# Opening of an mLSTM layer: operands by channel pairs, the prompt's norm factor inside the second range, the decay scans moved behind the key copies

## The chip, the cores and the metric

The kernel runs on one core of one Trainium2 chip. The metric is the device time of one execution in microseconds (us); of the kernel before there are three runs, 1829.74, 1832.8 and 1832.9 us, with a median of 1832.8 us.

## The reference

A two-layer encoder works on a prompt of 256 columns and a sample of 512 columns, in float32, with D = 1024 channels. Layer 0 mixes with a bidirectional mLSTM, layer 1 with windowed attention; behind each mixer stands a convolutional feed-forward net. Only the entry of layer 0 and, at its edge, the end of layer 1 bear on this change:

```
mod = silu(c) @ adaln_w[l] + adaln_b[l]            # shift, scale, gate, twice; one row per sequence
h   = rmsnorm(x, norm_g[l, 0]) * (1 + sc1) + sh1
proj = h @ w_in                                    # q, k, v, o and 16 gate rows
b    = cumsum(log_sigmoid(forget gate)); a = input gate - b
m    = running max of a                            # per direction, per head
s    = (q k^T) * exp(a_key - m_query), masked      # what the chunked scan computes in one piece
x    = x + g1 * (mixer(h) @ w_out); x = x + g2 * ffn(...)
return rmsnorm(x, final_g)
```

## The kernel before, in words

The T = 768 columns are held with channels on partitions: KC = 8 channel tiles of 128. They are worked on in three ranges of 256 columns: the sample's first half (columns 256 to 511, called r0 here), its second half (512 to 767, r1), and the prompt (0 to 255, r2). A matmul of float32 values is split: each operand is stored as a high part (fp32r, "hi") and the rest ("lo"), and a product tile is the sum of three products, hi·hi, lo·hi and hi·lo. In the trace `zh` and `zl` are the parts of the activations, `whi` and `wlo` those of the weights. A weight half is 512 KB: `raw` loads it on SP's queue, ScalarE casts `whi` (L272), VectorE subtracts to get `wlo` (L273).

`first` starts the program. SP's queue loads r0 of x, then sixteen 512 KB pieces of the adaLN weights with r1 of x and the gates' weights between them; the first four go to `raw` buffers, the others to slabs. `adaln` multiplies silu(c) with each piece (two matmuls per piece, L266, output `ps`), copies the result out on VectorE and ScalarE (L431, L432), turns it with four transposes (L435), and adds the bias (L442) to get shift and gain (L445). While that runs, `Norm` makes the factor of r0 and r1: ScalarE squares (L111, `nt`), GpSimd adds five of the eight squares up (L120), TensorE sums the three that remain over partitions (L266, `pa<-inv,nt`, two output columns per matmul), VectorE and GpSimd make the reciprocal root (L159, L160, `nr`), TensorE spreads it over partitions (`pa<-kct,nr`) and VectorE scales x in place (L571).

When the gain is there, `modulate` (L574) takes r0 and then r1: VectorE applies gain and shift in place (L578, eight instructions per range), ScalarE casts to `zh` (L272) and VectorE subtracts to `zl` (L273). Inside `mlstm` the prompt gets a `Norm` with `on_pe=KC`: no adding on GpSimd, all eight squares go to TensorE. Its factor is applied by `modulated` (L561, L563, L564). `window` (L323) then makes three output tiles over the three ranges in order, all eight channels of a tile before the next: the gate rows and the first two query tiles. The gates' output goes through ScalarE (L680, L681), the query tiles through `fp_copy_split` (L275, L276).

Behind the window the decay follows in program order: on ScalarE |f|, exp and ln (L700 to L702, with two table loads), on VectorE min and subtraction (L703, L704), four sums as scans (L707, L709), the subtraction L710 and four maxima as scans (L713, L714); then M is written to memory (L716, `mrows`) and read back broadcast over partitions (L732) for GpSimd to add the masks (L734). After that come the first head's keys (`gemmT`, U_MIN+1), its values (`gemmN`), the turning of `a` into columns (L723, L724), the exponentials E that need masks and columns (L793 to L797), and F+M (L813) with its exponential (L814). `adaln_v` spreads layer 1's modulation over VectorE (L516, L518, output `ada`) as fill work.

At the end of the program, layer 1's last product tiles are added to the residual (`resid`, L605), the last norm's factor is made, and `output` (L595 on VectorE) writes y.

A scheduler orders the instructions of each engine, except within `manual_schedule` blocks, where code order holds.

## Time and profile before

| what | value |
|---|---|
| median of three runs | 1832.8 us |
| profiled execution, its own time | 1832.56 us |
| its span, first to last instruction | 1830.8 us |
| mean granted TensorE clock | 0.989 |
| TensorE (PE) busy | 1789.2 us, 98% |
| VectorE (DVE) busy | 1379.1 us, 75% |
| ScalarE (ACT) busy | 893.0 us, 49% |
| GpSimd (POOL) busy | 483.8 us, 26% |

A row of the timeline reads: start and busy time in us, engine, line, operation, output<-inputs, shapes, how many instructions the row groups, and in brackets the idle time before it and what ended it. PEld is the loading of a matmul's stationary operand, which lies beside PE. In the windows view each row gives a stretch, its length, busy time and count of each engine, then the granted clock of TensorE, the DMA share and GB/s. Matmuls are pipelined, so a matmul's row is longer than the distance to the next one; the pace is read from starts.

### The profile page before, as it was taken

The numbers are of one execution on the slowest core, as the hardware profiler recorded it, in microseconds if no ns is written. First come the engines' busy times: TensorE is split into PE (matmuls) and PEld (weight loads), VectorE is DVE, ScalarE is ACT, GpSimd is POOL, SyncE is SP. The second block draws the span as 40 slices with busy tenths as digits, with TensorE's granted clock in tenths as the row PEclk, the third lists the DMA queues.
The fourth block names the chain that finished last, engine by engine and source line by source line (L and its number), as shares of the span: only waits on it lengthen the run. The fifth ranks groups of instructions, "written<-read, shape, count | busy, mean of one in ns | idle before, by whom it ended". The sixth has DMA issues, their size and how long they took to land.

```text
span 1830.8 us, 28867 instructions
## 1 busy us (share of the span) xinstructions
PE 1789.2 (98%) x11258; PEld 1653.6 (90%) x11258; DVE 1379.1 (75%) x2108; ACT 893.0 (49%) x1814; POOL 483.8 (26%) x385
## 2 busy tenths in 40 slices
PE   6999999999999999999999999999999999999998
PEld 3987887989998999999999999889989999999997
DVE  4755676886799877777777867767998777777876
ACT  4434434353556444444444566665564444444443
POOL 1001001022024333333331313430144333333321
PEclk7999999999999999999999999999999999999998
DMA  8344565546312222222222321124122222222212
GB/s 332 108 146 141 171 204 195 174 144 212 114 46 80 73 67 70 69 70 70 69 70 83 116 84 50 53 95 136 49 81 70 69 70 70 69 69 70 70 35 70
DMA packets 64244, 184.47 MB, mean 101 GB/s; under 512 B 6167, under 2 KB 23831, under 8 KB 64108
## 3 DMA queue, kind: packets, MB, share of 16 engines
q1 hardware_dynamic: 63532, 182.11, 30.3%
q8 instruction: 88, 1.44, 0.3%
q10 hardware_dynamic: 576, 0.52, 0.1%
q14 instruction: 48, 0.39, 0.1%
HBM read 176.17 MB, written 6.43 MB: 100 GB/s over the span
## 4 chain that ended last, share of the span: by engine, by line
PE 85%; DVE 5%; issue 4%; ACT 3%; DMA 1%; POOL 1%; SPq 0%; POOLq 0%; ACTq 0%; DVEq 0%
PE ps L266 27%; PE pa L266 24%; PE ps L1195 10%; PE ps L1196 10%; PE ps L1198 10%; PE pa L1034 1%; DVE wlo L273 1%; DMA slab<-in_adaln_w_dram 0%; DMA raw<-in_adaln_w_dram 0%; PE pa L1195 0%; PE pa L1196 0%; DVE ada L518 0%; ACT whi L272 0%; PE pa L1198 0%; ACT zh L1146 0%
## 5 line engine op out<-in xcount | busy, mean ns | idle before, releaser
L272 ACT CAST whi<-raw 128x1024 fp32r<-128x1024 f32 x233 | 243.8, 1049 | 332.5 <-PE pa L266 145.0
L273 DVE TENSOR_TENSOR wlo<-raw,whi 128x1024 fp32r<-128x1024 f32 x233 | 316.7, 1360 | 105.6 <-ACT whi L272 103.5
L266 PE MATMUL pa<-slab,whi 128*128 128x256 f32 (+1 forms) x1328 | 317.3, 334 | 0.0
L266 PEld LDWEIGHTS pa<-slab,whi 128*128 128x128 f32 x1328 | 230.1, 189 | 21.9 <-DVE slab L605 0.4
L605 DVE SCALAR_TENSOR_TENSOR slab<-pa,mod,slab 128x256 f32<-128x256 f32 (+1 forms) x332 | 192.7, 598 | 63.8 <-PE pa L266 63.6
L266 PE MATMUL pa<-slab,wlo 128*128 128x256 f32 (+1 forms) x664 | 212.8, 333 | 1.4 <-DVE wlo L273 1.4
L266 PE MATMUL ps<-zh,whi 128*128 128x256 f32 (+1 forms) x560 | 189.3, 339 | 2.6 <-ACT whi L272 1.9
L266 PE MATMUL ps<-zh,wlo 128*128 128x256 f32 (+1 forms) x560 | 184.1, 331 | 2.0 <-DVE wlo L273 2.0
L266 PE MATMUL ps<-zl,whi 128*128 128x256 f32 (+1 forms) x560 | 184.5, 332 | 0.5 <-DVE zl L564 0.5
L1195 PE MATMUL ps<-zh,whi 128*128 128x384 f32 x504 | 172.2, 342 | 3.8 <-ACT nt L1266 2.0
L1196 PE MATMUL ps<-zl,whi 128*128 128x384 f32 x504 | 169.9, 337 | 1.8 <-DVE zl L1152 1.8
L1198 PE MATMUL ps<-zh,wlo 128*128 128x384 f32 x504 | 169.0, 335 | 0.0
L266 PE MATMUL ps<-slab,whi 128*128 128x384 f32 (+2 forms) x656 | 163.5, 332 | 0.9 <-DVE slab L273 0.5
L266 PEld LDWEIGHTS pa<-slab,wlo 128*128 128x128 f32 x664 | 125.2, 189 | 14.3 <-DVE wlo L273 2.0
L1231 POOL TENSOR_TENSOR raw<-raw,raw 128x512 f32<-128x512 f32 x40 | 53.7, 1343 | 318.5 <-DVE wlo L273 245.8
L1447 POOL TENSOR_TENSOR slab<-slab 128x772 f32<-128x772 f32 x44 | 87.0, 1978 | 166.1 <-DVE slab L1435 154.1
L1434 DVE SCALAR_TENSOR_TENSOR slab<-slab,cstt,slab 128x771 f32<-128x771 f32 x88 | 108.9, 1239 | 26.7 <-ACT slab L1432 26.4
L266 PEld LDWEIGHTS ps<-zh,whi 128*128 128x128 f32 x560 | 107.6, 192 | 16.1 <-issue 4.4
L518 DVE SCALAR_TENSOR_TENSOR ada<-raw,silc,ada 128x1024 f32<-128x1024 f32 x84 | 110.6, 1354 | 14.6 <-DMA raw<-in_adaln_w_dram 14.4
L266 PEld LDWEIGHTS ps<-zl,whi 128*128 128x128 f32 x560 | 107.3, 192 | 12.6 <-issue 3.4
L266 PEld LDWEIGHTS ps<-slab,whi 128*128 128x128 f32 x656 | 115.2, 188 | 3.4 <-ACT whi L272 0.9
L266 PEld LDWEIGHTS ps<-zh,wlo 128*128 128x128 f32 x560 | 107.1, 192 | 12.2 <-DVE wlo L273 2.9
(295 smaller groups left out, 4292.8 us busy)
## 6 DMA issues: line engine op xcount, KB each, us to landing
raw<-in_w_dram SPq DMA_DIRECT2D x208, 512.0 KB, 3.7
raw<-in_adaln_w_dram SPq DMA_DIRECT2D x84, 512.0 KB, 4.5
slab<-in_x_dram SPq DMA_DIRECT2D x12, 512.0 KB, 6.7
slab<-in_adaln_w_dram SPq DMA_DIRECT2D x12, 512.0 KB, 10.3
slab<-mrows SPq DMA_DIRECT2D x8, 384.0 KB, 5.4
xs<-slab SPq DMA_DIRECT2D x6, 512.0 KB, 3.2
bt<-brow SPq DMA_DIRECT2D x16, 192.0 KB, 3.1
slab<-xs SPq DMA_DIRECT2D x6, 512.0 KB, 6.6
```

Of the source, the lines that this page charges most:

```text
L266: self.nc.tensor.matmul(out, lhsT, rhs, start=start, stop=stop)
L272: nc.scalar.copy(hi, src)
L273: return nc.vector.tensor_tensor(lo, src, hi.bitcast(F32), ALU.subtract)
L518: stt(acc[:, s], row, w, acc[:, s], ALU.mult, ALU.add)
L605: self.nc.vector.scalar_tensor_tensor(x, o, self.mod[l][:, gc + c, q : q + 1], x, ALU.mult, ALU.add)
L1034: nc.tensor.transpose(pp[:, ks], b.t[:, e, ks], self.ident)
L1195: mm(o, wh[:, k], hi[k], start=start and k == 0, stop=False, skip_group_check=True)
L1196: mm(o, wh[:, k], lo[k], start=False, stop=False, skip_group_check=True)
L1198: mm(o, wl[:, k], hi[k], start=False, stop=k == 3, skip_group_check=True)
L1231: tt(q[0], q[2], q[0], ALU.subtract)
L1434: stt(y[:, 1:], u[:, :-1], w(0), y[:, 1:], ALU.mult, ALU.add)
L1447: nc.gpsimd.tensor_tensor(y, y, yrow[:, j], ALU.mult)
```

## The change

1. `adaln` issues extra matmuls that multiply `ones` by `ones` into a bank that is overwritten later (`warm`): six behind the pieces of each of k = 3 to 6, one behind k = 7, five more behind the transposes. The two copies of the result go to two `tmp` buffers.
2. `modulate` is gone. `opening`, in which TensorE, ScalarE and VectorE follow the code's order, does r0, r1 and r2 for the three tiles. Gain and shift of even channels stay on VectorE, those of odd channels go to ScalarE. In r0 the gates and the first query tile advance by channel pairs, then the second query tile, then the lo parts of the weights. In r1 all three tiles advance by pairs. In r2 two tiles advance by channel and the third comes behind them. The prompt's eight squares are summed on GpSimd to one (`on_pe=0`), TensorE's four `pa<-inv,nt` rows stand ahead of the fifth channel of r1, the spreading ahead of the seventh.
3. The first half of the key weights is cast and subtracted at the end of `opening`; the first `adaln_v` row is issued behind that. The two raw loads of the first query weights stand ahead of the prompt's x on SP's queue.
4. The decay (L700 to L716) and the first head's `mrows` reads and masks are called inside `gemmN`, behind the value weights' split.
5. F+M waits to be issued until the low part of the third value tile has been issued.

TensorE's row order around the end of `adaln` (names: `ps_254` in the first and `ps_149` in the second is the bank of the transposes, `nt` are squares or the two copies, `ps_350` and `ps_310` the first product tile). Of before:

```order
L435 MATMUL ps_254<-kct,sb_251 128x128 x4
L266 MATMUL pa_375<-inv,nt_334 128x2
L266 MATMUL pa_375<-inv,nt_336 128x2
L266 MATMUL pa_375<-inv,nt_338 128x2
L266 MATMUL pa_375<-inv,nt_340 128x2
L266 MATMUL ps_350<-zh,whi_263 128x256
L266 MATMUL pa_375<-inv,nt_342 128x2
L266 MATMUL pa_375<-inv,nt_344 128x2
L266 MATMUL pa_375<-inv,nt_346 128x2
L266 MATMUL pa_375<-inv,nt_348 128x2
```

Of the change, from the fourth group of `warm` on:

```order
L266 MATMUL ps_149<-ones 128x128 x6
L432 MATMUL ps_148<-slab_260,silc 32x512 x4
L266 MATMUL ps_149<-ones 128x128
L445 MATMUL ps_149<-kct,nt_277 128x128 x2
L445 MATMUL ps_149<-kct,nt_278 128x128 x2
L266 MATMUL ps_310<-ones 128x128 x5
L266 MATMUL ps_310<-zh,whi_289 128x256
L266 MATMUL ps_310<-zh,wlo_290 128x256
L266 MATMUL ps_310<-zl,whi_289 128x256
```

The prompt's sixteen squares (one column block after the other) that stood around the first product are gone from this place, and the products follow each other from the first on.

VectorE's row order at the decay (`slab_315` and `slab_316` hold f, F, a and M before; `slab_293` and `slab_294` do in the change; `slab_665` and `slab_678` hold the keys). Of before:

```order
L273 TENSOR_TENSOR wlo_792<-raw_789,whi_791 128x1024
L707 SCALAR_TENSOR_TENSOR slab_316<-slab_315,slab_316 4x512
L709 SCALAR_TENSOR_TENSOR slab_316<-slab_315,slab_316 4x512
L707 SCALAR_TENSOR_TENSOR slab_316<-slab_315,slab_316 4x256
L276 SCALAR_TENSOR_TENSOR slab_318<-pa_612,slab_318 128x256
L709 SCALAR_TENSOR_TENSOR slab_316<-slab_315,slab_316 4x256
L710 TENSOR_TENSOR slab_316<-slab_315,slab_316 36x768
L713 SCALAR_TENSOR_TENSOR slab_316<-slab_316 4x512
L714 SCALAR_TENSOR_TENSOR slab_316<-slab_316 4x512
L713 SCALAR_TENSOR_TENSOR slab_316<-slab_316 4x256
L714 SCALAR_TENSOR_TENSOR slab_316<-slab_316 4x256
L813 TENSOR_TENSOR slab_316<-slab_316 36x768
```

Of the change:

```order
L273 TENSOR_TENSOR slab_678<-ps_679,slab_678 128x512
L528 SCALAR_TENSOR_TENSOR ada_911<-raw_970,silc,ada_911 128x1024
L707 SCALAR_TENSOR_TENSOR slab_294<-slab_293,slab_294 4x512
L709 SCALAR_TENSOR_TENSOR slab_294<-slab_293,slab_294 4x512
L273 TENSOR_TENSOR wlo_805<-raw_802,whi_804 128x1024
L707 SCALAR_TENSOR_TENSOR slab_294<-slab_293,slab_294 4x256
L709 SCALAR_TENSOR_TENSOR slab_294<-slab_293,slab_294 4x256
L273 TENSOR_TENSOR slab_678<-ps_706,slab_678 128x256
L273 TENSOR_TENSOR slab_678<-ps_739,slab_678 128x512
L710 TENSOR_TENSOR slab_294<-slab_293,slab_294 36x768
L273 TENSOR_TENSOR slab_678<-ps_766,slab_678 128x256
L713 SCALAR_TENSOR_TENSOR slab_294<-slab_294 4x512
```

The four copies of the keys stood behind all scans and the second value weights' subtraction; now they stand among the scans and ahead of the maxima, and the second value weights' subtraction (`wlo_805`) ahead of two of the sums.

VectorE's last rows (`slab` is x, `pa` the factor or a product tile). Of before:

```order
L159 TENSOR_SCALAR nr_17580<-pa_17573 128x2
L605 SCALAR_TENSOR_TENSOR slab_12431<-pa_17621,mod_89,slab_12431 128x256
L595 SCALAR_TENSOR_TENSOR slab_12430<-slab_12430,cstt,pa_17633 128x256 x2
L595 SCALAR_TENSOR_TENSOR slab_12431<-slab_12431,cstt,pa_17633 128x256 x4
L605 SCALAR_TENSOR_TENSOR slab_12431<-pa_17654,mod_89,slab_12431 128x256
L595 SCALAR_TENSOR_TENSOR slab_12430<-slab_12430,cstt,pa_17699 128x256 x3
L595 SCALAR_TENSOR_TENSOR slab_12431<-slab_12431,cstt,pa_17699 128x256 x3
```

Of the change:

```order
L159 TENSOR_SCALAR nr_17607<-pa_17600 128x2
L606 SCALAR_TENSOR_TENSOR slab_12458<-pa_17648,mod_89,slab_12458 128x256
L596 SCALAR_TENSOR_TENSOR slab_12457<-slab_12457,cstt,pa_17660 128x256 x2
L596 SCALAR_TENSOR_TENSOR slab_12458<-slab_12458,cstt,pa_17660 128x256 x2
L606 SCALAR_TENSOR_TENSOR slab_12458<-pa_17681,mod_89,slab_12458 128x256
L596 SCALAR_TENSOR_TENSOR slab_12458<-slab_12458,cstt,pa_17660 128x256 x2
L596 SCALAR_TENSOR_TENSOR slab_12457<-slab_12457,cstt,pa_17726 128x256 x3
L596 SCALAR_TENSOR_TENSOR slab_12458<-slab_12458,cstt,pa_17726 128x256 x3
```

No code was changed there; the last residual (now L606) has come to stand ahead of two of the six outputs.

Behind the first head's value products TensorE's order is the same as before, and so are VectorE's and ScalarE's behind the first turning of `a`, but for the rows above. SP's queue has the two query weight loads ahead of the prompt's x and one adaLN row ahead of the write of `mrows`; GpSimd has seven adds more.

The core of the diff:

```diff
     def adaln(self, l, th):
...
+            if h and k > 2:
+                with self.tc.issue_after(last.ins):
+                    self.warm(pt, 6 if k < KC - 1 else 1)
...
+        sb = [self.tmp([P, 256]) for _ in range(2)]
...
-    def modulate(self, xt, rng, l, i):
...
-        norm = Norm(self, xt, PROMPT, self.modulated(0, 0), KC)
...
-        self.window(ws)
+        self.opening(xt, gw, raws, (gates, keep(qt0, 0, 0), keep(qt0, 0, 1)))
...
-                self.gemmN(U_MIN + 3 * h + 2, evac)
+                self.gemmN(U_MIN + 3 * h + 2, evac, None if h else (decay, maxima))
...
-                nc.vector.tensor_tensor(F, F, M, ALU.add)
+                with self.tc.issue_after(self.third.ins):
+                    nc.vector.tensor_tensor(F, F, M, ALU.add)
...
+    def opening(self, xt, gw, raws, sinks):
...
+        norm = Norm(self, xt, r2, keep_factor, 0)
...
+            def made(c):
+                if c % 2:
+                    act(x(c), x(c), AF.Identity, scale=gain(c, q), bias=shift(c, q))
+                else:
+                    nc.vector.tensor_scalar(x(c), x(c), gain(c, q), shift(c, q), ALU.mult, ALU.add)
...
+        with self.tc.manual_schedule(engines={eng.PE, eng.Activation, eng.DVE}):
...
+            with self.tc.issue_after(self.turned.ins):
+                self.warm(bank[0, 0], 5)
+            high(0)
+            operands(r0)
+            high(1)
+            low(0)
+            low(1)
+            squares(0)
+            for c in range(0, KC, 2):
+                for k in (c, c + 1):
+                    three(r0, 0, k)
+                for k in (c, c + 1):
+                    mm(r0, 1, 0, 0, k)
+                    mm(r0, 1, 0, 1, k)
+            for c in range(KC):
+                mm(r0, 2, 0, 0, c)
+                mm(r0, 2, 0, 1, c)
+            for i in (1, 2):
+                for c in range(KC):
+                    mm(r0, i, 1, 0, c, c == KC - 1)
+            operands(r1, lambda: squares(4))
+            for c in range(0, KC, 2):
+                if c == 4:
+                    next(factor)
+                if c == 6:
+                    next(factor, None)
+                for i in range(3):
+                    for k in (c, c + 1):
+                        three(r1, i, k)
...
+            for c in range(KC):
+                if c + 1 < KC:
+                    ts[c + 1] = first(c + 1)
+                if c == 2:
+                    sinks[0](0, bank[0, 0])
...
+                three(r2, 0, c)
+                three(r2, 1, c)
+            for c in range(KC):
+                three(r2, 2, c)
+            self.opened = self.ahead(U_MIN + 1, 0)
```

More of the change, by code (lines that the diff above doesn't have):

```diff
@@ L297, in ahead @@
     def ahead(self, u, h):
-        self.early[u, h] = self.split(self.load(u, h))
+        hi, lo = (self.stg.tile([P, 1024], R, tag=t, name=self.nm(t), bufs=3) for t in ("whi", "wlo"))
+        self.early[u, h] = hi, lo
+        return self.fp_copy_split(hi, lo, self.load(u, h))
     def step(self, gen, n=1):
@@ L342, in window, with gemmN @@
                     consume(q, bank[i, q][:, : s1 - s0])
[L344 removed]
+    def gemmN(self, u, evac, then=None):
         ws = []
```

173 lines of the change are left out of this document (121 added, 52 removed).

## The prediction, made before the changed kernel ran

> **What bounds the kernel now.** The page comes first. Its first part says that TensorE is busy for 98% of the span and VectorE for 75%; its second part gives the granted clock in 40 slices.
>
> ```profile
> PE 1789.2 (98%) x11258; PEld 1653.6 (90%) x11258; DVE 1379.1 (75%) x2108; ACT 893.0 (49%) x1814; POOL 483.8 (26%) x385
> PEclk7999999999999999999999999999999999999998
> ```
>
> TensorE is the bound. The change leaves all products of the body, so it can win only where TensorE idles, does avoidable rows, or runs at a lower clock; the clock line puts that in the first slice. The windows view cuts the opening by granted clock, and the timeline of TensorE follows with what stands in those windows.
>
> ```profile
> 20.48:23.90 3.42, 1.05 (x4) 0.14 (x4) 2.05 (x1) 2.36 (x8) 2.64 (x4) 1.00 1.02 416
> 23.90:27.31 3.41, 3.27 (x11) 1.61 (x11) 0.00 (x0) 0.00 (x0) 0.98 (x2) 0.50 1.03 412
> 34.14:37.55 3.41, 2.68 (x21) 1.66 (x13) 2.06 (x9) 2.12 (x7) 0.00 (x0) 1.00 1.06 413
> 37.55:40.97 3.42, 3.33 (x15) 3.03 (x15) 3.42 (x12) 3.42 (x11) 0.00 (x0) 0.50 0.99 395
> 44.38:47.79 3.41, 3.41 (x18) 3.41 (x18) 3.41 (x8) 0.78 (x3) 0.98 (x1) 0.50 0.35 106
> ```
>
> ```profile
> 18.74 1.05 PE L266 MATMUL ps<-slab,silc 128*32 128x512 f32 x4 [0.24 <-DMA slab<-in_adaln_w_dram]
> 24.04 1.92 PE L266 MATMUL ps<-slab,silc 128*32 128x512 f32 x4 [0.24 <-DMA slab<-in_adaln_w_dram]
> ...
> 35.29 0.84 PE L435 MATMUL ps<-kct,sb 128*128 128x128 f32 x4 [0.56 <-DVE sb L431]
> 36.01 1.30 PE L266 MATMUL pa<-inv,nt 128*128 128x2 f32 x8
> 37.48 0.55 PE L266 MATMUL ps<-zh,whi 128*128 128x256 f32 x1 [0.18 <-ACT zh L272]
> 38.13 5.28 PE L266 MATMUL pa<-inv,nt 128*128 128x2 f32 x24
> 43.27 0.56 PE L266 MATMUL ps<-zh,whi 128*128 128x256 f32 x1
> ...
> 47.04 0.41 PE L266 MATMUL ps<-zl,whi 128*128 128x256 f32 x1
> 47.26 0.41 PE L266 MATMUL ps<-zh,wlo 128*128 128x256 f32 x1
> ...
> 71.56 0.40 PE L266 MATMUL ps<-zh,whi 128*128 128x512 f32 x1
> ```
>
> The reader sees: one product at 37.48, then 24 rows of the prompt's squares until 43.27, then products 0.215 us apart (47.04 to 47.26) while the clock is 0.50. The first key product, 71.56, ends the opening. The chain of waits gives the pace at full clock, 11.28/94 = 0.12 us:
>
> ```profile
> 51.81 11.28 PE ps L266 x94
> ```
>
> **The change, part by part.** The sum goes against the profiled execution's own 1832.56 us (span 1830.8, 1.76 around it), which lies 0.24 us under the median.
>
> *Squares leave TensorE.* From 37.48 to 43.27 are 5.79 us for one product; at 0.12 that leaves 5.67. Four summed rows return in the second range: 24 rows took 5.28 at half clock, so 0.22 each there; I take 0.12 each at full clock, 0.5. Term: **−5.2**. Lower bound −5.67; upper −4.8 with 0.22 a row.
>
> *Half clock.* From 43.27 to 47.79 some 21 products ran 0.215 apart; without the fall they cost 0.12: 21 × 0.095 = **−2.0**. It goes only if the first windows after adaLN stay at full clock. In these windows the squares look busy (3.33 of 3.42 from 37.55 on) yet the clock stays at 0.50 until the window from 44.38, full of products, is over: I read that rows of two columns do not count. In the change, products and the five `warm` fill these windows.
>
> *The end of adaLN.* The window from 20.48 holds 1.05 us of matmuls, and the next is granted 0.50. The `warm` matmuls add work there. Their row, `ones` of 128x128 in float32, has no like before except the spreading, a few rows at about the same size (four transposes in 0.84 above): 0.1 a row, 1.2 per group of six (two rows each), 2.4 at half clock. The first group starts near 19.8 and puts some 0.6 into the window from 20.48, which makes 1.6 of 3.41. Rows of before bracket that: 1.05 dropped the clock, 2.68 did as well if the squares' 1.30 are not counted (1.38), and the window from 143.36 (2.25) kept it. So both can happen. With full clock the last pieces, not TensorE, set the end:
>
> ```profile
> 33.01 0.45 PEld L266 LDWEIGHTS ps<-slab,silc 128*32 128x32 f32 x6 [0.42 <-DMA slab<-in_adaln_w_dram]
> 31.55 3.18 PE L266 MATMUL ps<-slab,silc 128*32 128x512 f32 x16
> 143.36:146.78 3.42, 2.25 (x24) 1.17 (x23) 0.65 (x2) 1.54 (x6) 1.92 (x2) 1.00 0.06 25
> 146.78:150.19 3.41, 1.87 (x17) 1.63 (x15) 1.92 (x3) 1.49 (x7) 2.67 (x2) 1.00 0.02 5
> ```
>
> The last piece has landed at about 33.0; with 1.05 for it the end is 34.1 instead of 34.73 (31.55 + 3.18), so −0.7. With one half-clock window from 23.90 on, the piece at 24.04 takes 1.92, the groups stand ahead of later pieces, and TensorE ends about 1.4 later. I take **+0.3**, near the middle. The Trainium skill, page "TensorE: Matmul & The Clock Gate", section "Part 1: The HAM clock gate (the "warmup" mystery)", says the clock falls after at least one idle window of about 3.4 us; the window from 20.48 was not idle, 1.05 us of it busy, and the trace shows the fall all the same. By that rule it would not fall at 23.90, the term would be −0.7, and the sum 1.0 lower.
>
> *Operands for the pairs.* VectorE and ScalarE must now keep ahead of TensorE.
>
> ```profile
> 36.38 0.25 DVE L445 SCALAR_TENSOR_TENSOR gain<-mod,cstt 128x8 f32<-128x8 f32 x2
> 36.58 5.26 DVE L578 TENSOR_SCALAR slab<-slab,gain,mod 128x256 f32<-128x256 f32 x16
> 41.76 2.43 DVE L273 TENSOR_TENSOR zl<-slab,zh 128x256 fp32r<-128x256 f32 x7
> 51.92 3.22 DVE L561 SCALAR_TENSOR_TENSOR nt<-slab,gain,pa 128x256 f32<-128x256 f32 x8 [2.38 <-issue]
> 56.38 3.25 DVE L564 SCALAR_TENSOR_TENSOR zl<-nt,mod,zh 128x256 fp32r<-128x256 f32 x8
> 38.90 1.61 ACT L272 CAST zh<-slab 128x256 fp32r<-128x256 f32 x5
> 37.66 1.33 ACT L111 ACTIVATE nt<-slab 128x256 f32<-128x256 f32 x4
> ```
>
> Per pair VectorE has one L578 (0.33) and two L273 (0.35 each), 1.0 us; ScalarE two casts (0.32) and one gain-and-shift, which no row shows, at least a square (0.33), at most a 0.41 instruction of VectorE (L561): 1.0 to 1.1. TensorE uses 10 products, 1.2 us, per pair of r0 and 18, 2.2 us, per pair of r1. Both engines keep up, though tightly in r0: first product 0.1 later, the first three channels 0.3. In r2 VectorE needs 0.40 + 0.41 = 0.81 per channel against 6 × 0.12 = 0.72, so 0.7 lost over eight channels, less what stands ready ahead; I take 0.3. Bounds: 0 if queues run ahead, 1.8 if every pair of r0 waits a further 0.25 and r2 loses 0.7. Term: **+0.7**. The key half's cast and subtraction at the end hide behind the third tile's 24 products (2.9 us); uncovered they would cost 2.3 (ScalarE 1.05, VectorE 1.22).
>
> *Behind the opening.* The first value product waited 0.44 for a key copy that stood behind the scans; in the order of the change that copy stands ahead of the maxima. Term: **−0.4**, bounds −0.44 and 0. The scans and masks move later, and what waits for them are the first exponentials:
>
> ```profile
> 88.83 0.38 PE L266 MATMUL ps<-whi,zh 128*128 128x256 f32 x1 [0.44 <-DVE slab L273]
> 85.04 0.68 DVE L714 TENSOR_TENSOR_SCAN slab<-slab 4x256 f32<-4x256 f32 x1
> 91.95 3.67 POOL L734 TENSOR_TENSOR slab<-slab,kct 128x768 f32<-128x768 f32 x2 [41.85 <-DMA slab<-mrows]
> 107.37 0.40 ACT L794 ACTIVATE E<-slab,aT 128x128 f32<-128x128 f32 x1 [0.59 <-DVE aT L724]
> ```
>
> Let E be the first key product. Before, the last scan ended at E + 14.2, the masks at 95.62, 9.9 later, and the first exponential ran at E + 35.8, after 11.7 us of slack. In the change the maxima stand behind the last key copy: E + 17.7, and four scans of 3.9 with adaLN rows between them, E + 22 to 24; masks at E + 32 to 34. Cost 0, with 1.5 to 3.5 us left.
>
> *The end.* The last residual stood behind six outputs on VectorE, though its product was done about 1818.3:
>
> ```profile
> 1817.89 0.41 PE L266 MATMUL pa<-slab,wlo 128*128 128x256 f32 x1
> 1817.47 2.44 DVE L595 SCALAR_TENSOR_TENSOR slab<-slab,cstt,pa 128x256 f32<-128x256 f32 x6 [2.19 <-ACT nt L587]
> 1819.83 0.48 DVE L605 SCALAR_TENSOR_TENSOR slab<-pa,mod,slab 128x256 f32<-128x256 f32 x1
> ```
>
> Behind four outputs it comes 2 × 0.40 earlier, and the last square, factor and outputs with it: **−0.7**; bounds −0.8 and 0.
>
> The sum: −5.2 − 2.0 + 0.3 + 0.7 − 0.4 − 0.7 = −7.3, and 1832.56 − 7.3 = **1825.3 us**. As a check, 216 products of the opening at 0.12 are 25.9 us; with 1.0 to the first product and 1.7 for other rows and waits, E comes 28.6 behind the gain (36.63), at 65.2, against 71.56 − 6.2 = 65.4 by the terms.
>
> **The rivals.** (a) *More half clock.* Each window at 0.50 costs 3.41 × 0.5 = 1.7 us of products. For it: windows with a little under half their time in matmuls fell. Against it: the opening is denser. One window gives 1827.0, two 1828.7. (b) *GpSimd's sum is late.* It has seven adds where it had five, and they must end before r1's fifth channel:
>
> ```profile
> 21.02 3.94 POOL L120 TENSOR_TENSOR nt<-nt,nt 128x256 f32<-128x256 f32 x5 [5.29 <-ACT nt L111]
> 28.89 0.71 POOL L160 TENSOR_TENSOR nr<-nr,mhalf 128x2 f32<-128x2 f32 x1 [3.93 <-DVE nr L159]
> 46.81 3.29 POOL L160 TENSOR_TENSOR nr<-nr,mhalf 128x2 f32<-128x2 f32 x1 [17.21 <-DVE nr L159]
> ```
>
> Alone an add takes 0.79, seven 5.5; but the small L160 took 3.29 instead of 0.71 while VectorE subtracted without pause. The four late squares are issued inside r1, some 8 us ahead of need; if each of their adds is stretched to 2.6, TensorE waits 1.5 to 3.7: 1826.8 to 1829.0. The Trainium skill, page "SBUF — State Buffer", section "Who interferes with whom", says that a VectorE instruction with two SBUF inputs contends with a GpSimd instruction that reads SBUF. The row at 46.81 agrees (3.29 against 0.71), and nearly half of VectorE's opening work is of that kind. (c) *Masks late.* If adaLN rows wait on their DMA among the scans, the slack goes and each further us is paid whole: up to 3, 1828.3. (d) *Slower.* Operands come one hand-off after another: per channel a product waits for gain, cast and subtraction in turn. With three instructions (0.33 + 0.32 + 0.35) and hand-offs of 0.1 as the waits around 37.48 show, a channel takes 1.3 to 1.5 us where queues do not run ahead. Over 24 channels this is 31 to 36 us against 25.9; from about 1.4 us a channel on the gain of 7.3 is eaten: 1833 to 1840. Against it: VectorE and ScalarE are issued two channels ahead. (e) *No change:* a later DMA wait swallows the gain; TensorE's 98% leaves little room: 1831 to 1833.
>
> **How the numbers follow.** Chances: the forecast 0.56 (own range 1823.3 to 1827.0), (a) 0.14, (b) 0.13, (c) 0.07, (d) 0.05, (e) 0.05. Leaving out (d), (e) and the far ends of (b) and (c) at the top, and at the bottom the sum of the lower bounds (−5.7, −2.0, −0.7, 0, −0.4, −0.8, in all −9.6: 1823.0) with 1.5 for the spread of the runs (1829.74 to 1832.9), the range is 1821.5 to 1829.2. A measurement of this kernel can tell about 0.2% from no change, 3.7 us, so faster means under 1829.1: all of the forecast and of (a), (b) and (c) nearly all, 0.88; same 0.07, slower 0.05.
>
> **What would show it.** Squares: no `pa<-inv,nt` rows between the transposes and the second product, and four inside r1. Clock: 1.00 from the first product on. Operands: little idle time between products to E, with VectorE named in r2. Sum: no wait for GpSimd at r1's fifth channel. Masks: the first exponential ended by the copy of `a`, not by GpSimd. End: the last residual about 0.7 earlier against the last product. The prediction is wrong if E lies beyond 68, or if the time behind E grows.

## The result and the profile after

The changed kernel takes 1827.8 us (median of 7 runs, 1825.02 to 1830.31) against 1832.8 us (7 runs, 1829.74 to 1835.66): a ratio of 0.9972, with a 95% interval of 0.9961 to 0.9983, or 5.1 us less. Measured again (experiment 5) the ratio was 0.9976 (0.9967 to 0.9984), 4.4 us. The forecast was 1825.3, 7.3 us less. The sign and the range hold; the forecast gain is 1.4 to 1.7 times the measured one, and lies above both intervals (3.1 to 7.1 and 2.9 to 6.0 us).

The profiled execution took 1826.64 us, with a span of 1824.9 and 1.74 around it; that is 5.9 under the profiled execution before. The page of the changed kernel, first and second part:

```profile
PE 1783.2 (98%) x11290; PEld 1649.6 (90%) x11290; DVE 1377.9 (76%) x2100; ACT 897.8 (49%) x1822; POOL 485.9 (27%) x392
PEclk9999999999999999999999999999999999999998
```

TensorE has 32 matmuls more and is busy 6.0 us less. The first digit of the clock is 9 where it was 7. The windows of the opening, in the changed kernel (length, busy time of PE, PEld, DVE, ACT and POOL, granted clock):

```profile
20.25:23.66 3.41, 1.80 (x12) 0.68 (x12) 1.62 (x1) 2.07 (x7) 2.90 (x4) 1.00 1.03 419
23.66:27.07 3.41, 3.41 (x28) 2.59 (x24) 0.00 (x0) 0.00 (x0) 0.73 (x1) 1.00 1.02 408
37.55:40.97 3.42, 3.42 (x27) 3.26 (x28) 3.11 (x9) 3.36 (x9) 0.00 (x0) 1.00 0.97 392
40.97:44.38 3.41, 3.41 (x30) 3.41 (x30) 2.92 (x5) 3.11 (x8) 1.30 (x1) 1.00 0.25 42
```

No window before 139 is at 0.50. TensorE's timeline, changed kernel:

```profile
33.44 1.09 PE L432 MATMUL ps<-slab,silc 128*32 128x512 f32 x8
34.46 0.49 PE L266 MATMUL ps<-ones 128*128 128x128 f32 x2
35.12 0.90 PE L445 MATMUL ps<-kct,nt 128*128 128x128 f32 x4 [0.18 <-DVE nt L442]
...
37.42 0.39 PE L266 MATMUL ps<-zh,whi 128*128 128x256 f32 x1 [0.28 <-ACT zh L937]
...
51.17 0.61 PE L266 MATMUL pa<-inv,nt 128*128 128x2 f32 x4 [0.20 <-POOL nt L120]
...
59.23 0.28 PE L266 MATMUL pa<-zl,whi 128*128 128x256 f32 x1
59.58 0.39 PE L266 MATMUL pa<-zh,whi 128*128 128x256 f32 x1
59.80 0.28 PE L266 MATMUL pa<-zh,wlo 128*128 128x256 f32 x1
60.10 0.38 PE L266 MATMUL pa<-zl,whi 128*128 128x256 f32 x1
...
65.85 0.40 PE L266 MATMUL ps<-zh,whi 128*128 128x512 f32 x1
```

The first product comes at the same time as before (37.42 against 37.48), the first key product at 65.85 instead of 71.56: 5.71 us earlier, nearly all of it gained between these two rows. Two kinds of loss are left. At 51.17 TensorE waits 0.20 for the last add on GpSimd (0.36 with the restart, from 50.69 + 0.12 to 51.17). In the prompt's range the starts are 0.35, 0.22 and 0.30 apart where 0.12 is the pace. ScalarE and VectorE show why:

```profile
57.76 0.67 ACT L681 ACTIVATE slab<-ps,cstt 36x512 f32<-36x512 f32 x1
58.44 0.69 ACT L682 ACTIVATE slab<-ps,cstt 36x512 f32<-36x512 f32 x1
59.03 0.90 ACT L1003 ACTIVATE zh<-nt,mod 128x256 fp32r<-128x256 f32 x2
59.56 0.48 DVE L1012 SCALAR_TENSOR_TENSOR zl<-nt,mod,zh 128x256 fp32r<-128x256 f32 x1 [0.68 <-ACT zh L1003]
```

The gates' output, 1.36 us of ScalarE, stands between two of the casts for which VectorE and then TensorE wait.

GpSimd's sum has a price on VectorE too. Of the gain-and-shift rows of the second range, one ran while GpSimd was idle and one beside its last four adds:

```profile
46.86 0.40 DVE L935 TENSOR_SCALAR slab<-slab,gain,mod 128x256 f32<-128x256 f32 x1
...
47.86 0.83 DVE L935 TENSOR_SCALAR slab<-slab,gain,mod 128x256 f32<-128x256 f32 x1
```

```profile
47.57 3.55 POOL L120 TENSOR_TENSOR nt<-nt,nt 128x256 f32<-128x256 f32 x4 [0.91 <-ACT nt L111]
```

The adds themselves took 0.9 to 1.2 us each here, 0.79 in the kernel before. TensorE's 18 products per pair cover the doubled rows in this range; experiments 3 and 12 show where they aren't covered.

Behind the opening, in the changed kernel:

```profile
87.71 0.68 DVE L714 TENSOR_TENSOR_SCAN slab<-slab 4x256 f32<-4x256 f32 x1
94.22 3.65 POOL L736 TENSOR_TENSOR slab<-slab,kct 128x768 f32<-128x768 f32 x2 [41.46 <-DMA slab<-mrows]
100.96 0.40 ACT L801 ACTIVATE E<-slab,aT 128x128 f32<-128x128 f32 x1 [0.59 <-DVE aT L724]
```

The last scan ends at 88.39, 22.5 behind the first key product, and the masks at 97.87, 32.0 behind it, with 3.1 us to spare: the first exponential is released by the copy of `a`, as forecast. It stands at 100.96 instead of 107.37, 6.4 earlier; that is 0.7 more than the opening gave, and 0.6 of it has come from the wait of the first value product, which stands 16.67 behind the first key product instead of 17.27.

The end, first VectorE's last outputs in the kernel before, then VectorE in the changed kernel, and then its view of DMA transfers over the last 8 us:

```profile
1824.96 2.44 DVE L595 SCALAR_TENSOR_TENSOR slab<-slab,cstt,pa 128x256 f32<-128x256 f32 x6 [4.66 <-PE pa L266]
```

```profile
1810.41 1.66 DVE L596 SCALAR_TENSOR_TENSOR slab<-slab,cstt,pa 128x256 f32<-128x256 f32 x4 [1.70 <-ACT nt L588]
1811.98 0.48 DVE L606 SCALAR_TENSOR_TENSOR slab<-pa,mod,slab 128x256 f32<-128x256 f32 x1
1817.12 2.44 DVE L596 SCALAR_TENSOR_TENSOR slab<-slab,cstt,pa 128x256 f32<-128x256 f32 x6 [3.88 <-PE pa L266]
```

```profile
q8 instruction: 1, 0.02, 0.7%
...
out_dram<-slab SPq DMA_DIRECT2D x4, 128.0 KB, 3.9
out_dram<-slab ACTq DMA_DIRECT2D x4, 128.0 KB, 3.9
```

The residual stands behind four outputs, and the last outputs begin at 1817.12, 7.84 earlier than before; the wait ahead of them is 3.88 instead of 4.66. But the span is only 5.9 shorter: the last eight writes landed 3.9 us after issue (1.8 in the kernel before), and an instruction load (`q8`, one packet of 16 KB) ran in the same microseconds.

### The profile page after: what moved, and what is told of

It reads as the page before. It is cut to its first block, busy times and chain, and to the rows that moved or that the text cites. A ratio compares the mean times of both kernels' runs of the same rounds, so it can differ in the third digit from the quotient of the medians.

```text
span 1824.9 us, 28936 instructions
## 1 busy us (share of the span) xinstructions
PE 1783.2 (98%) x11290; PEld 1649.6 (90%) x11290; DVE 1377.9 (76%) x2100; ACT 897.8 (49%) x1822; POOL 485.9 (27%) x392
## 4 chain that ended last, share of the span: by engine, by line
PE 85%; DVE 5%; issue 4%; ACT 3%; DMA 2%; POOL 1%; SPq 0%; POOLq 0%; DVEq 0%; ACTq 0%
PE ps L266 26%; PE pa L266 24%; PE ps L1339 10%; PE ps L1342 10%; PE ps L1340 10%; PE pa L1178 1%; DMA raw<-in_adaln_w_dram 1%; DVE wlo L273 1%; DMA slab<-in_adaln_w_dram 1%; PE pa L1339 0%; PE pa L1340 0%; ACT whi L272 0%; DVE wlo L1464 0%; PE pa L1342 0%; ACT zh L1290 0%
## 5 line engine op out<-in xcount | busy, mean ns | idle before, releaser
L606 DVE SCALAR_TENSOR_TENSOR slab<-pa,mod,slab 128x256 f32<-128x256 f32 (+1 forms) x332 | 192.8, 598 | 63.9 <-PE pa L266 63.8
L266 PE MATMUL ps<-zh,wlo 128*128 128x256 f32 (+1 forms) x560 | 180.3, 328 | 1.6 <-DVE wlo L273 1.6
L1591 POOL TENSOR_TENSOR slab<-slab 128x772 f32<-128x772 f32 x44 | 86.4, 1966 | 166.3 <-DVE slab L1579 148.6
L528 DVE SCALAR_TENSOR_TENSOR ada<-raw,silc,ada 128x1024 f32<-128x1024 f32 x84 | 112.3, 1372 | 11.9 <-DMA raw<-in_adaln_w_dram 11.8
```

Of the source, the lines that this page charges most:

```text
L266: self.nc.tensor.matmul(out, lhsT, rhs, start=start, stop=stop)
L528: stt(acc[:, s], row, w, acc[:, s], ALU.mult, ALU.add)
L606: self.nc.vector.scalar_tensor_tensor(x, o, self.mod[l][:, gc + c, q : q + 1], x, ALU.mult, ALU.add)
L1591: nc.gpsimd.tensor_tensor(y, y, yrow[:, j], ALU.mult)
```

## The experiments

Two moments serve as measures: the first product of the opening and the first key product. Times in us of the profiled executions; ratio to the kernel before as it was measured beside each.

| kernel | adaLN copied out | first product | first key product | between the two | ratio |
|---|---|---|---|---|---|
| before | 34.81 | 37.48 | 71.56 | 34.08 | 1 |
| before, again | 33.69 | 36.37 | 69.50 | 33.13 | one run |
| before, 16 small matmuls at the start | 35.63 | 38.30 | 72.25 | 33.95 | 1.0005 (0.9997 to 1.0014) |
| before, squares summed on GpSimd | 33.95 | 37.65 | 82.41 | 44.77 | 1.0078 (1.0066 to 1.0091) |
| before, decay later | 34.53 | 37.21 | 71.99 | 34.78 | 0.9995 (0.9986 to 1.0005) |
| changed | 34.65 | 37.42 | 65.85 | 28.43 | 0.9972 (0.9961 to 0.9983) |
| changed, again | 34.62 | 37.40 | 65.82 | 28.42 | 0.9976 (0.9967 to 0.9984) |
| changed, 28 small matmuls at the start | 34.69 | 37.47 | 65.88 | 28.41 | 0.9985 (0.9976 to 0.9994) |
| changed, without ones by ones | 33.74 | 36.51 | 64.92 | 28.41 | 0.9975 (0.9966 to 0.9985) |
| changed, squares on TensorE | 34.73 | 37.50 | 71.70 | 34.20 | 1.0005 (0.9996 to 1.0014) |
| changed, decay at its old place | 34.57 | 37.35 | 65.78 | 28.42 | 1.0004 (0.9994 to 1.0014) |
| changed, all gain and shift on VectorE | 34.66 | 37.39 | 67.63 | 30.24 | one run |
| changed, F+M free | 35.12 | 37.89 | 66.32 | 28.43 | one run |
| changed, three waits less | 34.20 | 36.98 | 64.81 | 27.83 | 0.9968 (0.9956 to 0.9980) |

**1 and 2. Small matmuls at the start.** They move the place of later instructions in TensorE's stream, 28 in the changed kernel, 16 in the one before. The edit of the first:

```diff
-        ps, pt = self.ps(), self.ps()
+        ps, pt = self.ps(), self.ps()
+        for _ in range(28):
+            self.mm(pt[:32, :2], self.ones[:, :32], self.inv, True, True)
```

> The changed kernel with 28 small extra matmuls (32x2) at the very start, where TensorE has nothing to do until the first adaLN piece lands; they only move all later instructions of TensorE back by about 112 places in its instruction stream. Theory 'instruction load': in the changed kernel the last 16 KB load of TensorE's instructions fell between the last writes of y (1819.93) and made them land 3.9 us after issue instead of 1.8. With 112 more instructions ahead that load comes before 1814, the last writes land in about 1.8 us, span 1822.9, and the time is about 2 us below the changed kernel, ratio to the kernel before 0.996. Rival 'the writes themselves': the earlier residual makes the writes collide with each other or with the queue whatever TensorE loads; then they land 3.9 us after issue again and the ratio stays at 0.997.

> The kernel before with 16 small extra matmuls (32x2) at the very start: about 64 more instructions in TensorE's stream, which makes its length that of the changed kernel. Theory 'instruction load': a last load of 16 KB now falls near the last writes, which land up to 2 us later; the time is 0 to 2 us above the kernel before, ratio 1.000 to 1.001, and one more instruction load (89 instead of 88) is seen. Rival 'the writes themselves': 88 or 89 loads, the last writes land in 1.8 us as in the kernel before, ratio 1.000.

In the first the writes landed in the usual time (the row below, against 3.9), the last instruction load came at 1806.5, and the end was 3.44 behind the last VectorE instruction instead of 5.29:

```profile
out_dram<-slab SPq DMA_DIRECT2D x4, 128.0 KB, 1.8
```

That is what the theory expected of the profile. But the times did not follow: 0.9985, not 0.996. In the second the 89th load came at 1832.36, behind the writes, which landed in 1.8; nothing could be told.

**3. The squares alone.** The kernel before, with the prompt's squares summed on GpSimd.

```diff
-        norm = Norm(self, xt, PROMPT, self.modulated(0, 0), KC)
+        norm = Norm(self, xt, PROMPT, self.modulated(0, 0), 0, wait=10.0)
...
+                with net.tc.issue_after(net.mark.ins):
+                    means()
```

> One part alone, on the kernel before: the prompt's squares are summed on GpSimd to one tile, and TensorE's four rows for it stand behind the fourth tile of the window; the order by tiles and the modulation of whole ranges on VectorE stay. Theory 'pairs are needed': TensorE then waits for the first zl, which VectorE makes only behind all sixteen gain-and-shift instructions (41.8), so the first key product comes only 1 to 2.5 us earlier than 71.56, ratio 0.999. Rival 'the squares were the cost' (the prediction's sum read literally): removing them gives 5.2 and the clock 2.0, first key product at 64.4, ratio 0.996.

It is 14 us slower, further than either theory. TensorE's waits in this kernel:

```profile
42.16 0.58 PE L272 MATMUL ps<-zh,whi 128*128 128x256 f32 x1 [4.12 <-ACT whi L278]
44.79 0.58 PE L272 MATMUL ps<-zl,whi 128*128 128x256 f32 x1 [2.05 <-DVE zl L279]
...
69.35 1.01 PE L272 MATMUL pa<-zh,whi 128*128 128x256 f32 x3 [4.70 <-ACT zh L569]
72.55 0.58 PE L272 MATMUL pa<-zl,whi 128*128 128x256 f32 x1 [2.19 <-DVE zl L570]
```

The first two (6.2 us) are the wait for operands that the squares had covered: ScalarE casts the weights' high part behind seven of the activations' casts and all eight squares, and VectorE modulates both ranges before the first `zl`. These sixteen gain-and-shift rows took 8.13 us here, with GpSimd's seven adds beside them, and 5.26 in the kernel before, where GpSimd was idle. The last two (6.9) come from the factor, which is spread only at 64.05, behind the window's fourth tile; two adaLN rows of VectorE (65.89 to 68.37) stand ahead of its first use. So TensorE's squares cost next to nothing by themselves in the old order, and about half of these waits come from the place that this experiment gave the factor. The gain needs the operands by pairs and a place for the factor.

**4. Without the matmuls of ones by ones.**

```diff
-                    self.warm(pt, 6 if k < KC - 1 else 1)
+                    pass
...
-                self.warm(bank[0, 0], 5)
+                pass
```

> The changed kernel without any of the extra matmuls of ones by ones. Theory 'they hold the clock': windows of 3.4 us at half clock come back between 24 and 34 and behind the end of adaLN, the first product starts 0 to 0.4 us later and one or two windows of products cost 1.7 each; first key product at 67.5 to 69.5 instead of 65.85. The last instruction load disappears (120 instructions fewer), which gives 2.0 back at the end; the last residual stands behind six outputs again, 0.8 lost. Sum +0.5 to +2.5 against the changed kernel, ratio to the kernel before 0.9975 to 0.9985. Rival 'they cost as much as they give': without them adaLN ends earlier by about 0.5, the clock is full once products run, first key product at 65.5 to 66.

The rival was right in the profile: adaLN is copied out at 33.74, 0.91 earlier, every window up to 144 is at 1.00, and the distance from the first product to the first key product is the same 28.41. The times do not differ (0.9975 here, 0.9976 for the changed kernel on the same chip); in this kernel the last residual stands behind six outputs again, which takes back 0.8. Over all profiles: of the seven with these matmuls none had a window at 0.50 before its first product, of the seven without them two had (the first of the kernel before and that of experiment 2). In the other five adaLN is copied out between 33.69 and 34.53, with these matmuls between 34.57 and 35.12. So they cost some 0.7 us; that they keep the clock up is not shown by two falls in seven.

**5. The changed kernel again.**

> The changed kernel again, unaltered, for a second profile and more times on this chip. Theory 'instruction load decides the end': its place in TensorE's instruction stream is fixed, so the last load again falls between 1815 and 1821 and the last writes land 3 to 4 us after issue; end 5.3 us behind the last VectorE instruction. Rival 'a chance of one execution': the load comes before 1815 or behind the writes, they land in 1.8 us, and the end is 3.4 us behind VectorE. In both cases the ratio is 0.997 to 0.998.

The rival came nearer: the load came at 1817.98, not before 1815, but the first of the last outputs began only at 1820.02, and the writes landed in 1.8. The late landing was a matter of one execution. At 1806 this execution is 0.7 us behind the first; then it loses 2.3 more in six microseconds. TensorE's squares of the last norm, first in the changed kernel's first profile, then in this one:

```profile
1808.02 1.40 PE L136 MATMUL pa<-inv,nt 128*128 128x2 f32 x12
```

```profile
1809.24 2.55 PE L136 MATMUL pa<-inv,nt 128*128 128x2 f32 x12
```

In the first the clock fell at 1811.6, here at 1807.9, ahead of these rows. The last 20 us hold many rows of two columns, and where the clock falls there differs between executions of one kernel (11.8 to 19.3 us ahead of the end in the profiles taken).

**6. Squares on TensorE at the new place.**

```diff
-        norm = Norm(self, xt, r2, keep_factor, 0)
+        norm = Norm(self, xt, r2, keep_factor, KC)
```

> The changed kernel with the prompt's eight squares on TensorE again (32 rows), but at the new place, ahead of the second range's fifth channel. Theory 'rows at their price': 32 rows of 0.12 instead of 4 and a wait of 0.2, first key product 3.1 us later, at 68.9. Rival 'rows of two columns do not hold the clock': the 3.8 us of them fill a window, the clock falls behind them for one or two windows and 1.7 to 3.4 more is lost, first key product at 70.5 to 72.5. If neither, and the first key product stays below 67, the squares were never a cost on TensorE.

TensorE's timeline and the windows around it:

```profile
50.88 4.55 PE L266 MATMUL pa<-inv,nt 128*128 128x2 f32 x32
55.28 0.56 PE L266 MATMUL ps<-zh,whi 128*128 128x256 f32 x1
```

```profile
50.00:53.40 3.40, 3.40 (x33) 3.40 (x31) 0.43 (x1) 0.29 (x1) 0.00 (x0) 0.99 0.00 0
53.40:56.80 3.40, 3.40 (x17) 3.40 (x18) 0.16 (x1) 0.00 (x0) 0.70 (x1) 0.50 0.00 0
```

The rows take 4.4 us, and a window that is busy for its whole length, three quarters of it with these rows, is followed by two at 0.50. The first key product comes 5.85 later, at 71.70, within the rival's 70.5 to 72.5: the rows at their price, and the clock behind them. That is the whole gain of the opening, and the ratio, 1.0005, says the same (0.8 us is lost at the end, where the last residual stands behind six outputs again).

**7. Decay at its old place.**

```diff
+        decay()
         aT = pool.tile([P, T6, G], F32, name="aT")
...
-                self.gemmN(U_MIN + 3 * h + 2, evac, None if h else (decay, maxima))
+                self.gemmN(U_MIN + 3 * h + 2, evac)
```

> The changed kernel with the decay and the masks called where they stood, ahead of the key projections. Theory 'the key copies were late': scans stand ahead of the key copies again, and the first value product comes 17.3 us behind the first key product as in the kernel before, instead of 16.7; 0.6 us lost, ratio 0.3 per mille above the changed kernel. Rival 'nothing rests on the order': 16.7 again, because in the new opening the scans end early enough.

Neither: 1.0004 against 0.9976, some 5 us lost and not 0.6 (0.8 of it at the end, where the last residual stands behind six outputs again). The opening is as fast as in the changed kernel (65.78), and then VectorE and TensorE show:

```profile
64.96 1.41 DVE L526 TENSOR_SCALAR ada<-raw,silc 128x1024 f32<-128x1024 f32 x2
...
74.34 2.47 DVE L528 SCALAR_TENSOR_TENSOR ada<-raw,silc,ada 128x1024 f32<-128x1024 f32 x2
...
85.86 0.68 DVE L714 TENSOR_TENSOR_SCAN slab<-slab 4x256 f32<-4x256 f32 x1
...
87.02 1.95 DVE L273 TENSOR_TENSOR slab<-ps,slab 128x512 fp32r<-128x512 f32 x4
```

```profile
82.73 0.56 PE L724 MATMUL pa<-kct,slab 36*128 36x36 f32 x6
83.22 1.66 PE L266 MATMUL pa<-slab,slab 128*128 128x512 f32 x6
87.01 0.73 PE L266 MATMUL pa<-slab,slab 128*128 128x512 f32 x2 [2.13 <-DVE slab L764]
87.77 0.39 PE L266 MATMUL ps<-whi,zh 128*128 128x256 f32 x1
```

The scans end at 86.5 here, 20.8 behind the first key product. With the old opening unaltered they end 14.2 behind it in each of four profiles (before 85.7, again 83.7, experiments 2 and 8 86.4 and 86.2). So the new opening itself lengthens the distance: the gates' last copy on ScalarE ends with the first key product (65.73) instead of 3.7 ahead of it, and six adaLN rows, 6.4 us of VectorE, stand between the opening and the scans; in the kernel before its adaLN rows had ended ahead of the first key product. The keys are finished 5.7 us earlier, but their copies still stand behind the scans (87.02).

TensorE, in this kernel, does the turning of `a` and eight of the first head's score products (`pa<-slab,slab`) ahead of the value products, and waits 2.13 among them; the first value product stands at 87.77, where in the changed kernel it stands at 82.52 with those rows still to come. A fair measure is the first `pa<-kct,hs` row, which turns the first head's output; behind it the kernels have the same number of matmuls left. It stands at 139.80 in the changed kernel, at 145.31 here and at 146.47 in the kernel before: 5.5 of the gain is gone by then. The wait at 87.01 is 2.1 of that; how the rest arises between there and this row is not shown.

**8. Decay later, alone.** The same edit on the kernel before.

```diff
-                self.gemmN(U_MIN + 3 * h + 2, evac)
+                self.gemmN(U_MIN + 3 * h + 2, evac, None if h else (decay, maxima))
```

> The other part alone, on the kernel before: the decay and the first head's masks are called behind the value weights, the opening stays. Theory 'the old opening hides the scans': the first key product comes as late as before, the scans are done by then, and at most the 0.44 wait of the first value product changes; ratio 0.9997 to 1.0003. Rival 'the decay is worth five microseconds by itself', as its undoing in the changed kernel cost: ratio 0.997.

The theory came nearer: 0.9995 lies just below its 0.9997 to 1.0003, and the interval (0.9986 to 1.0005) holds all of these and not the rival's 0.997. The first value product now comes 16.67 behind the first key product and not 17.27. So the edit is worth 0.6 by the profile on the old opening, and some 5 with the new one, in which it keeps the key copies from waiting for the scans.

**9. All gain and shift on VectorE.**

```diff
-                if c % 2:
-                    act(x(c), x(c), AF.Identity, scale=gain(c, q), bias=shift(c, q))
-                else:
-                    nc.vector.tensor_scalar(x(c), x(c), gain(c, q), shift(c, q), ALU.mult, ALU.add)
+                nc.vector.tensor_scalar(x(c), x(c), gain(c, q), shift(c, q), ALU.mult, ALU.add)
```

> The changed kernel with gain and shift of all channels of the first two ranges on VectorE, none on ScalarE. Theory 'VectorE's supply is close to the bound': per pair VectorE then has two times 0.33 and two times 0.40, 1.45 us, against 1.2 us of TensorE's products in the first range; TensorE waits some 0.25 per pair there and hides it in the second range; first key product 0.5 to 1.5 us later behind the first product (28.9 to 29.9 instead of 28.43). Rival 'ScalarE was the slower one': ScalarE's 0.60 per channel is gone, operands come sooner, the distance is 28.0 to 28.4.

The distance is 30.24, 1.8 more, above the 0.5 to 1.5 expected. Part of it stands in one row:

```profile
52.96 0.61 PE L266 MATMUL pa<-inv,nt 128*128 128x2 f32 x4 [1.06 <-POOL nt L120]
```

The other 0.9 are gaps between products of the first range and the first of the second. With all of it on VectorE, VectorE's supply is the bound there, and GpSimd's sum comes 0.9 later with it. The share on ScalarE is worth 1.8 in the opening.

**10. F+M free.**

```diff
-                with self.tc.issue_after(self.third.ins):
-                    nc.vector.tensor_tensor(F, F, M, ALU.add)
+                nc.vector.tensor_tensor(F, F, M, ALU.add)
```

> The changed kernel in which F+M need not wait for the third value tile. Theory 'no one waits': VectorE does it right behind the maxima, TensorE's distance from the first value product to the turning of a stays at 17.4 us and the first exponential at 18.4 behind the first value product. Rival: ScalarE's table load and exponential move between the copies of the value tiles and hold one up, 0.5 to 1.5 us more.

The distance from the first value product to the first exponential is 18.44 in both: this edit gives nothing.

**11. The kernel before again.**

> The kernel before again, unaltered, for a second profile. Theory 'the squares always bring the clock down': three windows of 0.50 begin at or shortly behind the first product, wherever the windows lie, and the first key product comes 33.9 to 34.1 us behind the first product, as in the first profile (34.08) and with 16 small matmuls at the start (33.95). The falls between 24 and 34 and in the last 20 us are a matter of where the windows lie and may differ. Rival 'the clock behind the squares is chance too': in this execution it stays at 1.00, and the distance is 29 to 31.5.

Two windows at 0.50 behind the squares, not three, and a distance of 33.13: near the theory, outside its numbers. TensorE's timeline and the windows around it:

```profile
32.59 1.05 PE L266 MATMUL ps<-slab,silc 128*32 128x512 f32 x4 [0.27 <-DMA slab<-in_adaln_w_dram]
...
37.01 4.53 PE L266 MATMUL pa<-inv,nt 128*128 128x2 f32 x24 [0.26 <-ACT nt L111]
```

```profile
38.37:41.78 3.41, 3.41 (x18) 3.41 (x18) 3.41 (x12) 3.41 (x11) 0.00 (x0) 0.50 0.83 329
41.78:45.19 3.41, 3.41 (x18) 3.41 (x18) 3.41 (x9) 2.27 (x6) 0.00 (x0) 0.50 0.01 4
45.19:48.60 3.41, 3.41 (x30) 3.41 (x30) 3.23 (x9) 0.00 (x0) 2.91 (x1) 1.00 0.61 179
```

The clock did not fall between 24 and 34 here; the last adaLN piece set the end, and the copy stands at 33.69, 1.12 ahead of the first profile. Each of the five profiles with the old opening (before, again, and experiments 2, 3 and 8) has a fall at 37.6 to 38.6, three windows long in four of them; in experiment 3, which has no square rows there, TensorE was idle for 4.12 instead.

**12. Three waits less.** The changed kernel without the matmuls of ones by ones, and:

```diff
-                if c == 2:
-                    sinks[0](0, bank[0, 0])
...
+            sinks[0](0, bank[0, 0])
             for c in range(KC):
                 three(r2, 2, c)
...
             squares(0)
+            squares(4)
...
-            operands(r1, lambda: squares(4))
+            operands(r1)
```

> The changed kernel without the matmuls of ones by ones, with the gates' output copied behind the third range's first two tiles instead of inside them, and with the last four of the prompt's squares right behind the first four on ScalarE. Theory: three waits go, each shown in the trace: 0.9 at the end of adaLN (33.74 instead of 34.65), 0.7 of TensorE waiting in the third range behind ScalarE's gate copies, 0.3 at the squares' rows. First key product at 63.9 instead of 65.85, last load absent, last residual behind six outputs (0.8 lost): span 1821.7, ratio to the kernel before 0.996. Rival 'the clock needs the extra matmuls': one or two half-clock windows in the opening, first key product at 65.5 to 67.5, ratio 0.998.

The two waits inside the opening went: no wait stands at the squares' rows, and the prompt's products start 0.12 apart without a gap. These were 1.1 us in the changed kernel (0.4 and 0.8). But the distance between the two products fell only from 28.42 to 27.83, because new gaps of 0.6 came in the second range, where all seven adds of GpSimd now run beside VectorE's first rows:

```profile
47.17 0.39 PE L266 MATMUL ps<-zl,whi 128*128 128x256 f32 x1 [0.26 <-DVE zl L938]
```

The first key product is 1.0 earlier than in the changed kernel, not 1.95. The other half of the shortfall is the end of adaLN, copied out at 34.20 and not 33.74; the first piece came 0.5 later in this execution than in experiment 4 (first matmul 9.93 and 9.42). The ratio is the lowest measured, 0.9968 against 0.9976 on the same chip, but the intervals overlap: faster than the kernel before, and not shown to be faster than the changed one.

## Why the prediction was right in direction and too large

*Squares leave TensorE (−5.2) and half clock (−2.0).* Right in place and together. From the first product to the first key product 34.08 became 28.43; putting the squares back at the new place costs 5.77 (experiment 6), some 3.6 of it rows (4.5 us between the products on either side instead of 0.95) and the rest clock. What the step left out is that the squares stood over a wait: taken away without the pairs (experiment 3) TensorE waits 6.2 us for operands at that place. The forecast had the pairs, so its sum held. The half clock is not the same in every execution: the second profile of before lost only two windows there and came to 33.13; over the four profiles with the old squares the mean distance is 34.0.

*The end of adaLN (+0.3).* Within its bounds, −0.7 and +1.4, against the profiled execution (copied out 0.16 earlier), but that execution of before was one in which the clock had fallen at 23.9. Where it does not fall, the copy stands at 33.69 to 34.53 without the change (again, experiments 3 and 8), and at 34.65 with it is 0.1 to 1.0 later. The rule of the Trainium skill that the prediction weighed (page "TensorE: Matmul & The Clock Gate", section "Part 1: The HAM clock gate (the "warmup" mystery)": a fall after an idle window) does not cover this: the window of 3.40 at 50.00 in experiment 6 was busy for all of its 3.40, with rows of two columns, and half clock followed.

*Operands for the pairs (+0.7).* The mis-sized term of the opening: 28.43 stands against 216 × 0.12 = 25.9 of products and 0.8 for eight other rows, so 1.7 were lost. The gaps between products give 0.4 in the first range, as forecast, 0.8 in the third range instead of 0.3, and 0.4 for GpSimd's sum, which the sum of terms had at nothing. In the third range the gates' copies on ScalarE are the cause shown (in experiment 12, with these copies behind the range's first two tiles, the gaps are gone); the prediction counted VectorE there and not ScalarE's other work. ScalarE's gain-and-shift, which the prediction put at 0.33 to 0.41, took 0.60 (L933), and VectorE's rows doubled beside GpSimd's adds.

*Behind the opening (−0.4 and no cost for the masks).* The masks were priced rightly: the scans end 22.5 behind the first key product, where E + 22 to 24 was forecast. The wait was −0.6. What the step left out is the price of not moving the decay: it took from the kernel before that the move is worth the wait of 0.44, while the new opening lengthens the distance from the first key product to the end of the scans from 14.2 to 20.8 at the old place. Without the move most of the gain, some 5 us, is lost again (experiment 7).

*The end (−0.7).* The order did it: 0.78. The wait ahead of the last outputs is 3.88 or 3.89 in the four profiles with the residual ahead of two outputs (changed, again, experiments 1 and 10), and 4.66 or 4.67 in the ten others. The late writes (1.9 in one execution) had no part in the forecast and are not in every execution.

So −6.4 up to the first exponential and −0.8 at the end stood in the first pair of profiles, nearly the −7.3 of the sum; the pair's execution times differ by 5.9. Against all four profiles of before and three of the changed kernel with the opening unaltered (before, again, experiments 2 and 8; changed, again, experiment 1) the first key product is 5.5 earlier on average (71.3 against 65.85) where 6.2 was forecast, and the time behind it 0.4 shorter (1759.4 and 1759.0) where 1.1 was: the spans are 5.9 shorter (1830.7 and 1824.9). Of the 0.7 missing behind the first key product the late writes of one execution are 0.6 in this mean. The clock in the last 20 us, which differed by 2.3 us between two executions of the changed kernel, moves each single profile. The 5.9 lies within both intervals of the measured ratio, the 7.3 outside; a further loss is not shown. Nor do the 28 small matmuls at the start need one: 0.9985 (0.9976 to 0.9994) and 0.9976 (0.9967 to 0.9984) overlap.

Of the rivals none came true: no fall in the opening (a), a wait of 0.2 for GpSimd's sum (b), whose adds were stretched to 0.9 to 1.2 and not to 2.6, masks with 3.1 us to spare (c), no slow hand-offs (d).

## What to carry to other kernels

Work on the bounding engine that stands over a wait costs only what it lasts beyond that wait; before it is taken away, ask what the engine will wait for in its place. A stage that ends earlier gains only if the next consumer does not hang on another chain, and the change itself can lengthen that chain: the scans ended 14.2 us behind the first key product with the old opening and 20.8 with the new one, and moving the key copies ahead of them was worth 0.6 us with the old and some 5 with the new. Work handed to an engine off the critical path can slow the one that supplies it: VectorE's rows took 0.83 instead of 0.40 beside GpSimd's adds. Where the clock depends on how windows of 3.4 us fall, take two profiles of the kernel before, and build the sum on what both show.

## What the runs showed of the hardware that was not expected

- Rows of two columns fill a window without holding the clock: 32 of them took 4.55 us, and the window that they filled for 2.5 us, busy for 3.40 of 3.40, was followed by two windows at 0.50 (experiment 6).
- VectorE's gain-and-shift of 128x256 took 0.40 with GpSimd idle and 0.83 beside GpSimd's adds in one range of the changed kernel, and the same in its second profile; sixteen of them took 8.13 instead of 5.26 in experiment 3.
- The same kernel's clock falls in some executions and not in others, with the same work: between 24 and 34 us in the first profile of before (three windows) and not in the second, and 20.0 or 15.2 us of half clock at the end of the changed kernel.
- One load of 16 KB of TensorE's instructions, 0.92 us long, while the last eight writes of 128 KB were under way, went with a landing 3.9 us after issue instead of 1.8. When it ran 2 us earlier (experiment 5) the writes were not late.
